# The last level of a block-triangular inverse on 64 x 64 blocks, and packed Q tiles, in a gated delta rule

## The chip, the cores and the metric

The kernel runs on one core of a Trainium2 chip. The metric is the device time of one execution in microseconds; a lower one is better. TensorE (PE) multiplies, VectorE (DVE), ScalarE (ACT) and GpSimd (POOL) work on tiles in on-chip memory, and PE writes its results into PSUM, eight banks of which the other engines read.

## What is computed

An attention layer, a feed-forward layer, a token mixer and a second feed-forward layer, over 512 tokens of 1024 features, all in float32. The change is in the mixer, in its gated delta rule. It has 8 heads of 128 features, and for each head and chunk of tokens a unit lower triangular system is solved:

```python
kk = jnp.einsum('nbhik,nbhjk->nbhij', kc, kc)
a_mat = jnp.where(strict, bc[..., :, None] * kk * decay, 0.0)
rhs = jnp.concatenate([bc[..., None] * vc, (bc * jnp.exp(gc))[..., None] * kc], axis=-1)
sol = lax.linalg.triangular_solve(a_mat + eye, rhs, left_side=True, lower=True,
                                  unit_diagonal=True)
...
def step(S, xs):
    q_i, qk_i, u_i, w_i, k_i, gl_i = xs
    v_new = u_i - jnp.einsum('bhck,bhkv->bhcv', w_i, S)
    o_i = jnp.einsum('bhck,bhkv->bhcv', q_i, S) + jnp.einsum('bhij,bhjv->bhiv', qk_i, v_new)
    S = S * jnp.exp(gl_i)[..., None, None] + jnp.einsum('bhck,bhcv->bhkv', k_i, v_new)
    return S, o_i
```

Ahead of it stand a causal convolution of width 4 and a SiLU over q, k and v; behind it a norm, a gate and projections.

## The kernel before

The large projections are products in which each float32 operand is split into a high and a low part, three matmuls for one (`acc<-hT,whi`, `acc<-hT,wlo` in the trace). They run all through the mixer. Between them a planner (`later`, `spend`, `run_until`) puts the small steps of the delta rule: each step that is set up gets a due time on a clock that the planner adds up from the matmuls issued so far, and is issued when that time has come. The table `DL` holds the delays: 10 us from U's first form to the first level of the inverse (`U`), 3.5 us between its steps (`lev`). That sets the program order, which PE keeps. The order on the other engines is set by a scheduler that looks at the whole program and moves instructions within an engine.

The kernel takes the tokens in 4 chunks of 128 (NT = 4). For each head, `decays` and `exps` make the decay matrices E and ET, `products` and `products2` the norms and E, the strictly triangular matrix of the system (L1119). `substitution` inverts its 16 x 16 diagonal blocks on DVE (shuffles into La, products pr, sums xs), and `expand` writes them into U, a tile of 128 x 512 with the four chunks side by side (L1169). `inverse(lev)` then joins neighbouring blocks of size s = 16, 32 and 64 into blocks of twice the size. A level has these steps: four matmuls with the chunk of E as the weights, onto the odd blocks' columns of U; DVE multiplies the result by a mask and writes Q (L1186); four transposes of U (L95) and their copy to X by ACT (L1190); then in `second` four matmuls of X and Q, and DVE subtracts them from U (L1195). A float32 matmul appears in the trace as two records, so `sc<-U,E x8` is four matmuls; a transposition is one.

Q of each level is a tile of its own, `Q_[lev]`, cleared once at the start of the mixer; the columns between the odd blocks stay zero. X comes anew from the work pool, which has 61 places of 128 x 512 (`self.tile`). The masks lie in `cst`, read from memory by one transfer. Around the inverse of head h stand the work of head h + 1, among it `ev_conv`: ACT copies a projection to cvr and scales it to cvy, DVE adds three taps (L1048, widths 511, 510 and 509), and ACT applies the SiLU (L1050).

Of the kernel before, what the change touches and what calls it, by code (L numbers as in the profile page):

```python
# [12 lines left out]
ALU = mybir.AluOpType  # L13
AX = mybir.AxisListType

P = 128
S = 512
NT = S // P
# [15 lines left out]
DL = dict(ada=21.24, qk=11.18, p0=10.0, wt=6.0, o=14.0, U=10.0, hn=7.73, lev=3.5, ch=2.2, cs=25.33, po=13.74, pr=18.0, T=3.17, la=6, gs=4, gp=5, Ts=6.12, P2=150)  # L34
# [7 lines left out]
class Net:  # L42
# [607 lines left out]
    def attention_layer(self):  # L650
# [17 lines left out]
        def qk(g, which):  # L668
# [17 lines left out]
            def evict(t, bank):  # L686
# [4 lines left out]
                ss = sp.tile([P, 8], F32, tag="ss8", name="ss8")  # L691
                nc.vector.tensor_reduce(ss, sq.rearrange("p (h d) -> p h d", d=64), axis=AX.X, op=ALU.add)
                r = self.rstd(ss, 8, 64)
# [58 lines left out]
        def attn(g, total):  # L752
# [48 lines left out]
            def weigh(h, b, wt, rs):  # L801
# [13 lines left out]
                ss = sp.tile([P, NT], F32, tag="ss4", name="ss4")  # L815
                nc.vector.tensor_reduce(ss, sq.rearrange("p (b n) -> p b n", b=NT), axis=AX.X, op=ALU.add)
                r = self.rstd(ss, NT, P)
# [136 lines left out]

    def mixer(self):
        nc, a, sp = self.nc, self.a, self.sp
        H = 8
        win = a["mix_w_in_2"][0]
        C = self.const
        sl = lambda t: slice(t * P, (t + 1) * P)  # L960
        ch = lambda x: x.rearrange("p (t n) -> p t n", t=NT)
# [1 line left out]
        small = lambda name, n=NT: sp.tile([P, n], F32, tag=f"sm{n}", name=name, bufs=24 if n == NT else 4)  # L963

        cst = self.tile("cst")
        nc.gpsimd.dma_start(cst[:, :448], a["k_mix"])
        tri, bmask = cst[:, 0:128], cst[:, 128:256]
        mq = [cst[:, 256 + 64 * i:320 + 64 * i] for i in range(3)]
        cols, rows = self.cols, self.rows
        cw = cols[:, 11:107].rearrange("p (j n) -> p j n", j=4)  # L970
        dng, psc, delta0, rcnt_ = cols[:, 107:108], cols[:, 108:112], cols[:, 112:128], cols[:, 128:192]
        alog, dtb = rows[:, 256:264], rows[:, 264:272]
        Q_ = [self.tile(f"Q{i}") for i in range(3)]
        for q in Q_:
            nc.gpsimd.memset(q, 0.0)


        G = lambda name: C.tile([P, H, NT], F32, name=name)
        beta, gc, egc = G("beta"), G("gc"), G("egc")
        gdram = self.dram.tile([H, S], F32, name="gdram")  # L980
        fl = lambda x: x.rearrange("p h t -> p (h t)")
# [7 lines left out]
        def ba_trans(ba):  # L989
# [10 lines left out]
            nc.vector.reciprocal(beta, e)  # L1000
            nc.vector.tensor_tensor(y, v[:, 8:16, :], dtb.unsqueeze(2).broadcast_to([P, H, NT]), op=ALU.add)
            nc.vector.tensor_scalar(t1, y, 0.0, None, op0=ALU.min)
# [15 lines left out]
            nc.gpsimd.tensor_tensor(ea, work[:, 192:200], alog, op=ALU.pow)  # L1018
            nc.vector.scalar_tensor_tensor(y, y, -1.0, ea.unsqueeze(2).broadcast_to([P, H, NT]), op0=ALU.mult, op1=ALU.mult)

# [37 lines left out]
        def mm4(out, a_, b_, t0=0, cols=lambda x: x):  # L1058
            for t in range(t0, NT):
                self.mm(cols(out[:, sl(t)]), a_[:, sl(t)], cols(b_[:, sl(t)]))  # L1060

        def delta(h):
            yq, yk, yv = conv_out[h], conv_out[8 + h], conv_out[16 + h]
            d = {}
# [22 lines left out]
            def products():  # L1087
# [6 lines left out]
                nc.scalar.activation(sq, trk, AF.Square)  # L1094
                nc.vector.tensor_reduce(ssq[:, NT:], ch(sq), axis=AX.X, op=ALU.add)
                trq = self.bank("sc")
                self.transpose4(trq, lambda t: yq[:, sl(t)])
                sq = self.tile("sq")
                nc.scalar.activation(sq, trq, AF.Square)
                nc.vector.tensor_reduce(ssq[:, 0:NT], ch(sq), axis=AX.X, op=ALU.add)  # L1100
                nc.vector.tensor_scalar(ssq, ssq, EPS, None, op0=ALU.add)
# [36 lines left out]
            def substitution():  # L1138
# [4 lines left out]
                Ac = sp.tile([P, NT, 16], F32, tag="Ac", name="Ac", bufs=1)  # L1143
                nc.vector.tensor_reduce(Ac, tmp.rearrange("p (t b j) -> p t j b", t=NT, b=8), axis=AX.X, op=ALU.add)
                La = [self.tile("La").rearrange("p (i t j) -> p i t j", i=8, t=NT) for _ in range(2)]
# [20 lines left out]
                def expand():  # L1166
                    U = self.tile("U")
                    b8 = lambda x, n: x.unsqueeze(n).broadcast_to([P, NT, 8, 16])
                    nc.vector.tensor_tensor(U.rearrange("p (t b i) -> p t b i", t=NT, b=8), b8(xs, 2),  # L1169
                                            b8(bmask.rearrange("p (b i) -> p b i", b=8), 1), op=ALU.mult)  # L1170
                    d["U"] = U
                    self.later(DL["U"], lambda: inverse(0))
# [2 lines left out]

            def inverse(lev):

                s = 16 << lev
                odd = lambda x: x.rearrange("p (u two s) -> p u two s", two=2, s=s)[:, :, 1, :]
                A, U, Q = d["E"], d["U"], Q_[lev]  # L1180
                qp = self.bank("sc")
                mm4(qp, A, U, cols=odd)
                na = 4 // (1 << lev)
                msk = mq[lev].rearrange("p (a s) -> p a s", s=s).unsqueeze(1).broadcast_to([P, NT, na, s])
                v4 = lambda x: x.rearrange("p (t a two s) -> p t a two s", t=NT, two=2, s=s)[:, :, :, 1, :]
                nc.vector.tensor_tensor(v4(Q), v4(qp), msk, op=ALU.mult)  # L1186
                xp = self.bank("sc")
                self.transpose4(xp, lambda t: U[:, sl(t)])
                X = self.tile("X")
                nc.scalar.copy(X, xp)  # L1190

                def second():
                    up = self.bank("sc")
                    mm4(up, X, Q, cols=odd)
                    nc.vector.tensor_tensor(odd(U), odd(U), odd(up), op=ALU.subtract)  # L1195
                    self.later(DL["lev"], (lambda: inverse(lev + 1)) if lev < 2 else weights)

                self.later(DL["lev"], second)

# [62 lines left out]
        def zcol(h):  # L1262
            og_[h] = self.tile("z")
            self.gemm_col(win[:, 3584 + h * P:3584 + (h + 1) * P], KD, self.hmov,
                          lambda bank: nc.scalar.activation(og_[h], bank, AF.Silu))
# [37 lines left out]
        def yacol(n):  # L1303
            self.gemm_col(a["pool_proj_2"][0, :, n * P:(n + 1) * P], 4, lambda k: yT[k],
                          lambda bank: nc.vector.tensor_tensor(m1[n], bank, m1[n], op=ALU.mult))

        cols = (4608, 512, 512 + 1024, 512 + 2048)
# [12 lines left out]
        zcol(0)  # L1320
        for h in range(H):
            if h:
# [15 lines left out]
        for n in range(KD):  # L1338
            yacol(n)
        self.run_until(lambda: st["og"] == H)  # L1340
        oT = [self.hp.tile([P, KD, S], F32R, tag=f"hT{i}", name=f"oT{i}") for i in range(2)]
# [55 lines left out]
def constants():  # L1397

    import numpy as np

    p = np.arange(P)[:, None]
    f = np.arange(P)[None, :]
    d = p + (S - P) - np.arange(S)[None, :]
    def pairs(s):
        m = (p // s % 2 == 0) & (f // s == p // s + 1)
        return m.reshape(P, -1, 2, s)[:, :, 1, :].reshape(P, 64)

    c = {
        "k_ident": p == f,
        "k_d3": np.where(d >= 0, -d, NEG),  # L1410
        "k_mix": np.concatenate([p <= f, p // 16 == f // 16] + [pairs(s) for s in (16, 32, 64)], 1),
    }
    return {n: np.ascontiguousarray(v.astype(np.float32)) for n, v in c.items()}

# [36 lines left out]
```

## Time and profile before

| | us |
|---|---|
| median of 3 runs | 1855.97 |
| lowest and highest run | 1852.57, 1855.99 |
| the profiled execution | 1854.37 |
| its span, first to last instruction | 1852.6 |
| PE busy in the span | 1811.6 |
| DVE, ACT, POOL busy | 1405.9, 934.2, 409.2 |

The mean granted TensorE clock of the execution is 0.996 of full speed. The time of an execution is its span and 1.8 us around it. The mixer's inverses lie between 1056 and 1350 us. In the timeline a row gives the start, the time from the start of the first to the end of the last of its instructions, the engine, the line, the operation with what it writes and reads, and how many there were; in square brackets stands for how long the engine sat idle ahead of it and who ended that. Ends of matmuls are modelled and overlap the next ones, so distances between starts are the safer reading.

### The profile page before, as it was taken

The page shows a single profiled execution, that of the slowest core. Times are in us where ns is not written, and L with a number is a line of the kernel's source. Part 1 is how long each engine was busy: PE and PEld are TensorE (multiplying, and loading weights), DVE is VectorE, ACT ScalarE, POOL GpSimd, SP SyncE. Part 2 cuts the span into 40 slices and gives each one's busy share as a digit, 9 for nine tenths or more (in the row PEclk, how much of TensorE's full clock was granted, in tenths as well). Part 3 has the DMA queues.
Part 4 walks back from the last instruction along what each step waited for, and adds up shares of the span by engine and source line. Part 5 has one row for each costly group of instructions (what it writes and reads, how often), then busy time and mean ns, then how long its engine had stood idle before and what let it go on. Part 6 is the DMA issues. An engine that isn't in the chain of part 4 may idle for free. (4 is left out here: it accounts for less than half of the span.)

```text
span 1852.6 us, 29069 instructions
## 1 busy us (share of the span) xinstructions
PE 1811.6 (98%) x10799; PEld 1598.0 (86%) x10799; DVE 1405.9 (76%) x2904; ACT 934.2 (50%) x1696; POOL 409.2 (22%) x396
## 2 busy tenths in 40 slices
PE   8999999999999999999999999999999999999997
PEld 5888888888888999998898778888888899999886
DVE  5558777777856899998365798787868789999833
ACT  5576676475743544453245745654433254445421
POOL 3213124042102123232030212212110022322201
PEclk9999999999999999999999999999999999999999
DMA  4535544535422233357324321222357323333731
GB/s 171 136 107 144 161 120 126 188 92 154 133 86 73 69 115 95 112 187 234 114 62 121 88 65 52 63 63 77 100 170 231 117 69 114 94 113 103 228 103 57
DMA packets 186594, 217.93 MB, mean 118 GB/s; under 512 B 9619, under 2 KB 129827, under 8 KB 186453
## 3 DMA queue, kind: packets, MB, share of 16 engines
q1 hardware_dynamic: 178864, 192.68, 34.6%
q0 software_dynamic: 6864, 22.27, 3.9%
q8 instruction: 85, 1.39, 0.3%
q10 hardware_dynamic: 724, 1.12, 0.2%
q14 instruction: 57, 0.46, 0.1%
HBM read 201.34 MB, written 2.11 MB: 110 GB/s over the span
## 5 line engine op out<-in xcount | busy, mean ns | idle before, releaser
L84 PE MATMUL acc<-hT,whi 128*128 128x256 f32 (+1 forms) x2704 | 639.9, 330 | 0.6 <-DVE hT L107 0.5
L84 PEld LDWEIGHTS acc<-hT,whi 128*128 128x128 f32 x2704 | 445.5, 191 | 33.4 <-DVE hT L107 0.7
L84 PE MATMUL acc<-hT,wlo 128*128 128x256 f32 (+1 forms) x1352 | 440.3, 326 | 3.0 <-DVE wlo L107 2.9
L106 ACT CAST whi<-raw 128x1024 fp32r<-128x1024 f32 (+1 forms) x325 | 285.7, 880 | 296.3 <-PE acc L84 232.2
L107 DVE TENSOR_TENSOR wlo<-raw,whi 128x1024 fp32r<-128x1024 f32 (+1 forms) x325 | 330.5, 1027 | 132.1 <-ACT whi L106 130.6
L84 PEld LDWEIGHTS acc<-hT,wlo 128*128 128x128 f32 x1352 | 257.5, 190 | 26.1 <-DVE wlo L107 4.2
L84 PE MATMUL acc<-whi,hT 128*128 128x512 f32 x768 | 264.9, 403 | 1.9 <-ACT hT L106 1.9
L84 PE MATMUL acc<-whi,gs 128*128 128x512 f32 x704 | 219.6, 390 | 1.6 <-DVE gs L107 1.6
L305 POOL TENSOR_TENSOR rs<-ms,mhalf 128x8 f32<-128x8 f32 (+2 forms) x60 | 86.2, 1438 | 447.5 <-DVE ms L303 388.0
L84 PE MATMUL acc<-T,whi 128*128 128x256 f32 x960 | 174.5, 283 | 0.0
L84 PEld LDWEIGHTS acc<-whi,hT 128*128 128x128 f32 x768 | 144.1, 188 | 32.1 <-ACT hT L106 2.9
L84 PEld LDWEIGHTS acc<-whi,gs 128*128 128x128 f32 x704 | 132.0, 188 | 29.9 <-DVE gs L107 2.5
L106 ACT CAST whi<-S 128x512 fp32r<-128x512 f32 x160 | 99.4, 621 | 115.2 <-DVE S L232 87.7
L84 PE MATMUL acc<-wlo,hT 128*128 128x512 f32 x384 | 150.5, 392 | 2.8 <-DVE wlo L584 2.8
L84 PEld LDWEIGHTS acc<-T,whi 128*128 128x128 f32 x960 | 149.8, 192 | 0.0
L107 DVE TENSOR_TENSOR wlo<-S,whi 128x512 fp32r<-128x512 f32 x160 | 140.1, 895 | 0.2 <-ACT whi L106 0.2
L84 PE MATMUL acc<-wlo,gs 128*128 128x512 f32 x352 | 137.1, 389 | 0.0
L84 PE MATMUL acc<-T,wlo 128*128 128x256 f32 x480 | 135.8, 283 | 0.0
L232 POOL TENSOR_TENSOR S<-raw,S 128x512 f32<-128x512 f32 x40 | 65.7, 1643 | 200.7 <-DVE S L232 158.6
L780 ACT ACTIVATE p<-p,mn 128x128 f32<-128x128 f32 (+3 forms) x128 | 71.1, 557 | 48.8 <-DVE mn L776 48.2
L84 PEld LDWEIGHTS acc<-T,wlo 128*128 128x128 f32 x480 | 92.2, 192 | 0.0
L84 PEld LDWEIGHTS acc<-wlo,hT 128*128 128x128 f32 x384 | 72.5, 189 | 14.7 <-DVE wlo L584 3.7
(299 smaller groups left out, 3113.6 us busy)
## 6 DMA issues: line engine op xcount, KB each, us to landing
raw<-in_ffn_w_in_dram SPq DMA_DIRECT2D x88, 512.0 KB, 3.6
raw<-in_l_w_in_dram SPq DMA_DIRECT2D x60, 512.0 KB, 4.1
raw<-in_mix_w_in_dram SPq DMA_DIRECT2D x53, 512.0 KB, 3.9
araw<-in_ada_w_dram SPq DMA_DIRECT2D x96, 256.0 KB, 4.3
raw<-in_ffn_w_out_dram SPq DMA_DIRECT2D x44, 512.0 KB, 3.7
ada<-in_ada_w_dram POOLq DMA_DIRECT2D x48, 256.0 KB, 4.2
raw<-in_l_w_out_dram SPq DMA_DIRECT2D x16, 512.0 KB, 3.7
ab<-in_ada_b_dram POOLq DMA_DIRECT2D x18, 256.0 KB, 4.2
```

The costliest lines, as they stand in the source:

```text
L84: self.nc.tensor.matmul(out, a, b, start=start, stop=stop, skip_group_check=onto)
L106: return (self.nc.scalar.copy(hi, src), self.nc.vector.tensor_tensor(lo, src, hi.bitcast(F32), op=ALU.subtract))
L107: self.nc.vector.tensor_tensor(lo, src, hi.bitcast(F32), op=ALU.subtract))
L232: sub = lambda o, x, y, op=ALU.subtract, e=nc.vector: e.tensor_tensor(o, x, y, op=op)
L305: pin(nc.gpsimd.tensor_tensor(r[:, :n], ms[:, :n], self.mhalf[:, :n], op=ALU.pow))
L780: nc.scalar.activation(p_[m][:, :L], p_[m][:, :L], AF.Exp, bias=mn[:, m:m + 1], scale=-1.0, accum_out=st[:, m, b:b + 1])
```

## The change

The first two levels stay in `inverse(lev)`, but Q and X both come from the work pool, and Q is packed: the odd blocks of a chunk lie side by side, 64 columns for each chunk, 256 in all. The three tiles Q_ and their clearing on POOL go.

The last level is a new function, `inverse_halves`. With the rows and columns of a chunk cut into a low and a high half, it multiplies the lower left quarter of E with the lower right quarter of U (64 x 64 weights, 64 columns), copies the result to Q without a mask, transposes the upper left quarter of U alone, and subtracts the product from the upper right quarter of U. Its tiles are 64 x 256. The third mask is no longer read.

```diff
@@ -954,7 +954,7 @@
 
     def mixer(self):
         nc, a, sp = self.nc, self.a, self.sp
-        H = 8
+        H, H2 = 8, P // 2
         win = a["mix_w_in_2"][0]
         C = self.const
         sl = lambda t: slice(t * P, (t + 1) * P)
@@ -963,16 +963,13 @@
         small = lambda name, n=NT: sp.tile([P, n], F32, tag=f"sm{n}", name=name, bufs=24 if n == NT else 4)
 
         cst = self.tile("cst")
-        nc.gpsimd.dma_start(cst[:, :448], a["k_mix"])
+        nc.gpsimd.dma_start(cst[:, :384], a["k_mix"])
         tri, bmask = cst[:, 0:128], cst[:, 128:256]
-        mq = [cst[:, 256 + 64 * i:320 + 64 * i] for i in range(3)]
+        mq = [cst[:, 256 + 64 * i:320 + 64 * i] for i in range(2)]
         cols, rows = self.cols, self.rows
         cw = cols[:, 11:107].rearrange("p (j n) -> p j n", j=4)
         dng, psc, delta0, rcnt_ = cols[:, 107:108], cols[:, 108:112], cols[:, 112:128], cols[:, 128:192]
         alog, dtb = rows[:, 256:264], rows[:, 264:272]
-        Q_ = [self.tile(f"Q{i}") for i in range(3)]
-        for q in Q_:
-            nc.gpsimd.memset(q, 0.0)
 
 
         G = lambda name: C.tile([P, H, NT], F32, name=name)
@@ -1175,25 +1172,52 @@
 
             def inverse(lev):
 
-                s = 16 << lev
+                s, na = 16 << lev, 4 >> lev
                 odd = lambda x: x.rearrange("p (u two s) -> p u two s", two=2, s=s)[:, :, 1, :]
-                A, U, Q = d["E"], d["U"], Q_[lev]
+                A, U = d["E"], d["U"]
+                Q, X = self.tile("Q")[:, :NT * H2], self.tile("X")
+                v4 = lambda x: x.rearrange("p (t a s) -> p t a s", t=NT, s=s)
+                q = lambda x, t: x[:, t * H2:(t + 1) * H2].rearrange("p (a s) -> p a s", s=s)
                 qp = self.bank("sc")
-                mm4(qp, A, U, cols=odd)
-                na = 4 // (1 << lev)
+                for t in range(NT):
+                    self.mm(q(qp, t), A[:, sl(t)], odd(U[:, sl(t)]))
                 msk = mq[lev].rearrange("p (a s) -> p a s", s=s).unsqueeze(1).broadcast_to([P, NT, na, s])
-                v4 = lambda x: x.rearrange("p (t a two s) -> p t a two s", t=NT, two=2, s=s)[:, :, :, 1, :]
-                nc.vector.tensor_tensor(v4(Q), v4(qp), msk, op=ALU.mult)
+                nc.vector.tensor_tensor(v4(Q), v4(qp[:, :NT * H2]), msk, op=ALU.mult)
                 xp = self.bank("sc")
                 self.transpose4(xp, lambda t: U[:, sl(t)])
-                X = self.tile("X")
                 nc.scalar.copy(X, xp)
 
                 def second():
                     up = self.bank("sc")
-                    mm4(up, X, Q, cols=odd)
+                    for t in range(NT):
+                        self.mm(odd(up[:, sl(t)]), X[:, sl(t)], q(Q, t))
                     nc.vector.tensor_tensor(odd(U), odd(U), odd(up), op=ALU.subtract)
-                    self.later(DL["lev"], (lambda: inverse(lev + 1)) if lev < 2 else weights)
+                    self.later(DL["lev"], (lambda: inverse(lev + 1)) if lev < 1 else inverse_halves)
+
+                self.later(DL["lev"], second)
+
+            def inverse_halves():
+
+                A, U = d["E"], d["U"]
+                Q, X = (self.tile(n)[:H2, :NT * H2] for n in ("Q", "X"))
+                lo, hi = slice(0, H2), slice(H2, P)
+                h = lambda x, t: x[lo, t * H2:(t + 1) * H2]
+                qp, xp = self.bank("sc"), self.bank("sc")
+                for t in range(NT):
+                    self.mm(h(qp, t), A[hi, sl(t)][:, lo], U[hi, sl(t)][:, hi])
+                nc.vector.tensor_copy(Q, qp[lo, :NT * H2])
+                for t in range(NT):
+                    nc.tensor.transpose(h(xp, t), U[lo, sl(t)][:, lo], self.ident[lo, lo])
+                    self.now += 0.06
+                nc.scalar.copy(X, xp[lo, :NT * H2])
+
+                def second():
+                    up = self.bank("sc")
+                    for t in range(NT):
+                        self.mm(h(up, t), h(X, t), h(Q, t))
+                    u = ch(U)[lo, :, hi]
+                    nc.vector.tensor_tensor(u, u, up[lo, :NT * H2].rearrange("p (t n) -> p t n", t=NT), op=ALU.subtract)
+                    self.later(DL["lev"], weights)
 
                 self.later(DL["lev"], second)
 
@@ -1408,7 +1432,7 @@
     c = {
         "k_ident": p == f,
         "k_d3": np.where(d >= 0, -d, NEG),
-        "k_mix": np.concatenate([p <= f, p // 16 == f // 16] + [pairs(s) for s in (16, 32, 64)], 1),
+        "k_mix": np.concatenate([p <= f, p // 16 == f // 16] + [pairs(s) for s in (16, 32)], 1),
     }
     return {n: np.ascontiguousarray(v.astype(np.float32)) for n, v in c.items()}
```

DVE at the start of head 1's work, where head 0 is in the first level of its inverse. Before, Q of head 0 stands first; E, abd, kd, Ac, kt, cvy and La are head 1's:

```order
L1186 TENSOR_TENSOR Q_10010<-sc,cst 128x16x16
L1085 TENSOR_TENSOR er<-cvy,er 128x512
L1095 TENSOR_REDUCE ssqk<-sq 128x4
L1100 TENSOR_REDUCE ssqk<-sq 128x4
L1101 TENSOR_SCALAR ssqk<-ssqk 128x8
L1119 SCALAR_TENSOR_TENSOR E<-sc,b_11008,E 128x128 x4
L1142 TENSOR_TENSOR abd<-E,cst 128x512
L1125 TENSOR_TENSOR kd<-kt,ekd 128x512
L1144 TENSOR_REDUCE Ac<-abd 128x64
L1126 TENSOR_TENSOR kt<-kt,bB 128x512
L1048 SCALAR_TENSOR_TENSOR cvy<-cvr,cols,cvy 128x511
L1153 STREAM_SHUFFLE La<-Ac 128x64
```

After, from the second convolution tap of the same stretch on (the E x4, abd, kd, Ac, kt and the first tap stand ahead of these rows as they did before):

```order
L1150 STREAM_SHUFFLE La<-Ac 128x64
L1045 SCALAR_TENSOR_TENSOR cvy<-cvr,cols,cvy 128x510
L1150 STREAM_SHUFFLE La<-Ac 128x64
L1045 SCALAR_TENSOR_TENSOR cvy<-cvr,cols,cvy 128x509
L1150 STREAM_SHUFFLE La<-Ac 128x64
L1185 TENSOR_TENSOR Q<-sc,cst 128x256
L1150 STREAM_SHUFFLE La<-Ac 128x64 x12
L1158 TENSOR_TENSOR pr<-La,xs 128x4x7
L1158 TENSOR_TENSOR pr<-La,xs 128x4x8
L1194 TENSOR_TENSOR U<-U,sc 128x16x16
```

Q has moved from ahead of E to behind the third tap (128x509), and the subtraction from U stands behind the rest of the shuffles and two products.

ACT at the same place, before. X belongs to head 0, cvr, cvy and vb to head 1:

```order
L1044 COPY cvr<-acc 128x512
L1046 ACTIVATE cvy<-acc,cols 128x512
L1190 COPY X<-sc 128x512
L1135 ACTIVATE vb<-sc,bv 128x128 x4
L1050 ACTIVATE cvy<-cvy 128x512
L106 CAST whi<-raw 128x1024
```

And after:

```order
L1041 COPY cvr<-acc 128x512
L1043 ACTIVATE cvy<-acc,cols 128x512
L1047 ACTIVATE cvy<-cvy 128x512
L1188 COPY X<-sc 128x512
L1132 ACTIVATE vb<-sc,bv 128x128 x4
L106 CAST whi<-raw 128x1024
```

The copy to X stands behind the SiLU of cvy (the line of 128x512 without cols), which was two rows behind it.

PE at the third level of head 0, before; the first two rows of U are the first half of the level:

```order
L95 MATMUL sc<-ident,cvy 128x128 x8
L84 MATMUL sc<-U,E 128x64 x4
L95 MATMUL sc<-ident,U 128x128 x4
L84 MATMUL acc<-hT_9847,whi 128x512
L84 MATMUL acc<-hT_9848,whi 128x512
L84 MATMUL acc<-hT_9847,wlo 128x512
```

After:

```order
L95 MATMUL sc<-ident,cvy 128x128 x8
L84 MATMUL sc<-U,E 64x64 x4
L1210 MATMUL sc<-ident,U 64x64 x4
L84 MATMUL acc<-hT_9847,whi 128x512
L84 MATMUL acc<-hT_9848,whi 128x512
L84 MATMUL acc<-hT_9847,wlo 128x512
```

The same number of instructions stands there, on 64 x 64 blocks. Up to here PE's order is that of before, with the packed forms of Q in the first two levels.

## Rows read from the trace of the kernel before

**Rows 1.** The page: engines' busy us (share of the span) and instructions

```profile
PE 1811.6 (98%) x10799; PEld 1598.0 (86%) x10799; DVE 1405.9 (76%) x2904; ACT 934.2 (50%) x1696; POOL 409.2 (22%) x396
```

**Rows 2.** PE's waits, 1000 to 1400 us: releaser, then total us, times, longest

```profile
PE sc L84 <- DVE U L1169: 2.7, 1, 2.7
PE sc L84 <- DVE Q L1186: 2.2, 2, 1.9
PE sc L84 <- DVE U L1195: 2.1, 1, 2.1
```

**Rows 3.** Windows: PE, PEld, DVE, ACT, POOL busy, granted clock, DMA, GB/s

```profile
1058.40:1061.80 3.40, 3.40 (x11) 2.81 (x12) 1.84 (x4) 2.02 (x4) 1.44 (x1) 0.50 0.56 154
1072.00:1075.50 3.50, 3.50 (x13) 3.02 (x13) 3.50 (x12) 0.56 (x2) 0.00 (x0) 0.51 0.53 143
1096.10:1099.50 3.40, 3.36 (x22) 3.11 (x23) 3.40 (x34) 1.52 (x3) 0.00 (x0) 1.00 0.00 0
```

**Rows 4.** Timeline of PE, head 0: start, us, instruction, [idle before <-releaser]

```profile
1056.74 1.08 PE L84 MATMUL sc<-U,E 128*128 128x64 f32 x8 [2.68 <-DVE U L1169]
...
1063.89 1.00 PE L84 MATMUL sc<-Q,X 128*128 128x64 f32 x8
...
1068.68 0.39 PE L84 MATMUL acc<-hT,wlo 128*128 128x512 f32 x1
1071.20 1.22 PE L84 MATMUL sc<-U,E 128*128 128x64 f32 x8 [2.14 <-DVE U L1195]
```

**Rows 5.** Timeline of DVE at the same place

```profile
1057.86 0.42 DVE L1186 TENSOR_TENSOR Q<-sc,cst 128x256 f32<-128x256 f32 x1
...
1062.63 1.13 DVE L1119 SCALAR_TENSOR_TENSOR E<-sc,b,E 128x128 f32<-128x128 f32 x4 [2.36 <-POOL b L1107]
...
1068.16 0.74 DVE L1048 SCALAR_TENSOR_TENSOR cvy<-cvr,cols,cvy 128x509 f32<-128x509 f32 x1
```

**Rows 6.** Timeline of ACT at the same place

```profile
1059.79 0.63 ACT L1190 COPY X<-sc 128x512 f32<-128x512 f32 x1
...
1068.99 0.63 ACT L1050 ACTIVATE cvy<-cvy 128x512 f32<-128x512 f32 x1 [5.49 <-DVE cvy L1048]
```

**Rows 7.** Timeline of PE at head 0's third level

```profile
1083.51 1.00 PE L84 MATMUL sc<-U,E 128*128 128x64 f32 x8
...
1084.72 0.71 PE L84 MATMUL acc<-hT,whi 128*128 128x512 f32 x2
...
1089.25 1.00 PE L84 MATMUL sc<-Q,X 128*128 128x64 f32 x8
1090.07 0.71 PE L84 MATMUL acc<-hT,whi 128*128 128x512 f32 x2
```

**Rows 8.** Timeline of PE at two small tiles (16 rows, then 32 columns)

```profile
961.02 0.40 PE L84 MATMUL acc<-hT,whi 128*128 128x256 f32 x2
961.26 0.28 PE L84 MATMUL acc<-hT,wlo 128*128 128x256 f32 x1
961.47 0.42 PE L992 MATMUL sc<-ident,ba 16*128 16x16 f32 x4
...
962.16 0.28 PE L84 MATMUL acc<-hT,wlo 128*128 128x256 f32 x1
...
990.10 0.62 PE L84 MATMUL acc<-hT,whi 128*128 128x512 f32 x2
990.56 0.40 PE L84 MATMUL acc<-hT,wlo 128*128 128x512 f32 x1
990.79 0.27 PE L1030 MATMUL sc<-ident,gc 128*32 128x128 f32 x1
...
991.37 0.40 PE L84 MATMUL acc<-hT,wlo 128*128 128x512 f32 x1
```

**Rows 9.** PE's loads at the 16-row tile: timeline, then line L992 (ns min/median/max)

```profile
961.47 0.32 PEld L992 LDWEIGHTS sc<-ident,ba 16*128 16x128 f32 x4
...
L992 PEld LDWEIGHTS sc<-ident,ba x4: 133/137/138, 961.5 to 961.6; 16*128 16x128 f32 x4
```

## The prediction

> **What bounds the kernel now.** First the busy times of the engines: TensorE (PE) is busy for 98% of the span [rows 1], so what counts is the work that PE does and the moments at which it waits; DVE, ACT and POOL have idle time, and a longer or shorter instruction of theirs counts only where PE waits for it. So the next view is the list of PE's waits over the stretch in which all eight heads are inverted (1000 to 1400 us). Three lines name the inverse: 2.7 us for the first U, 2.1 us for the U of the next level, 2.2 us for a Q, of which 1.9 in one wait [rows 2]. All of them lie in heads 0 and 1. After that, up to the last head, the list holds almost nothing: from head 2 on the inverse is covered by projection matmuls, and only PE's own work in it is on the path.
>
> Third, the table of windows, for the granted clock. In the 3.4 us after the 2.7 us wait the granted clock is 0.50 (1.2 GHz in place of 2.4), in the 3.5 us after the 2.1 us wait 0.51, and after the 1.9 us wait it stays 1.00 [rows 3]. So each of the two longer waits also costs about half of the window behind it, 1.7 us: PE did in 3.4 us what takes 1.7 at 1.00.
>
> Last the timeline around head 0. PE runs the first U x E at 1056.74, Q x X at 1063.89 without waiting, projection matmuls until 1069.07 (5.18 us from the start of Q x X), then waits and goes on with the second level at 1071.20 [rows 4].
>
> **The change, part by part.** *The order of DVE and ACT at head 0.* PE keeps its order up to the third level of head 0, but the other engines' order comes from the scheduler, and there the change moves two instructions a long way. Q of the first level is evicted by DVE at 1057.86 before, as an early instruction; after, it stands behind the whole start of head 1 (the four E, abd, kd, Ac, kt and three convolution taps). On ACT, X is copied at 1059.79 before; after, it stands behind the SiLU of the convolution, which waits for the third tap. Whether the scheduler does so because the tile Q now has to be found in the work pool I can't tell from the order; that it does is what counts, since the queue of each engine is worked off in order. The third tap ran at 1068.16 for 0.74 and the SiLU behind it for 0.63 from 1068.99 [rows 5, 6]. The taps stand behind E, which waited for POOL; without the 0.42 us of Q in front, the two reductions that POOL waits for come 0.4 earlier, so I take the third tap to end at 1068.5, the SiLU at 1069.15 and X (0.63 [rows 6]) at 1069.75; Q is done by then (1068.5 + 0.42 = 1068.9). PE, which stands at Q x X at 1063.89, goes on at about 1069.8: **a new wait of 5.9 us**. Behind it on PE are queued the projection matmuls, which need nothing from DVE, and nothing on PE can pass it.
>
> What is late next? The second level needs U, which DVE subtracts behind the remaining twelve shuffles and two products; DVE is there at about 1071.3 and the product of Q and X has been done since 1070.7, while PE has its 5.18 us of projections to do until 1075.0. So the 2.14 us wait at 1071.20 is gone. PE starts the second level at 1075.0 in place of 1071.20, 3.8 us late. Before, the half clock behind the 2.14 us wait then cost 1.7 us; that goes with the wait: 3.8 - 1.7 = 2.1. The new wait of 5.9 us is longer than both that were followed by a half clock, so I charge it one such window, +1.7 (0 to 1.7). **Order at head 0: +3.8 us** (2.1 to 5).
>
> *Later heads.* At head 1, PE waited 1.9 us for Q [rows 2]; DVE is still the later one there, and what feeds DVE at that place comes from PE and POOL and shifts with PE. I take the wait as unchanged. From there to head 2 the order puts Q and U somewhat later on DVE than before relative to PE (3 to 7 us, when its instructions are laid out with the durations of before), in a stretch with waits of none to 0.5 us. I charge 0.5 us, between 0 and 2.5 (one more wait of the size of the 1.9 us one, with a bit). From head 3 on the order of DVE is no later than before.
>
> *PE's work in the third level.* Before, it is 8 records of U x E and 4 transposes from 1083.51 to 1084.72, 1.21 us, and 8 records of Q x X from 1089.25 to 1090.07, 0.82 us [rows 7]: 2.03 us per head for 20 records, 0.10 each. The records are the same in number after, with weights of 64 rows by 64 columns in place of 128 by 128 and, for the transposes, 64 columns moving in place of 128. The trace has no such operation. The nearest rows on the low side are the four 16-column transposes of the gates, whose loads follow each other every (0.32 - 0.137) / 3 = 0.061 us [rows 9]; on the high side, the pitch stays at 0.10. I take 0.06, since both the loaded columns and the moving ones are fewer or equal: 1.2 us per head, **a saving of 0.8** (0 to 1.0, the latter for half of 0.10).
>
> Against this stand two visits per head to a smaller tile of the array. The trace has two such visits. At the gates the time from one wlo record to the next around four 16-row transposes is 962.16 - 961.26 = 0.90, of which three records of 0.12 are normal; 0.54 remain, less four transposes at 0.061 to 0.10: 0.14 to 0.30 for going there and back. At the transposition of gc, with 32 columns, 991.37 - 990.56 = 0.81, less three records at 0.23 and one transposition at 0.10: 0.02 [rows 8]. A 64 x 64 tile narrows rows and columns, so I take the row with fewer rows as nearest, 0.25 per visit, 0.5 per head, with 0.02 and 0.30 as the ends. A rule of the Trainium skill ("TensorEngine Tiling (Array Packing)", Tiling Modes, Key Properties) says that changing the tiling mode, not the tile alone, drains TensorE. The first of the two visits agrees with it, the second shows nearly no drain. By the rule at the larger price the saving per head would be 0.2, by the second visit 0.8.
>
> Net per head: 0.8 - 0.5 = 0.3. Head 0's is lost, since PE waits for DVE at head 1; seven heads give **-2.1 us**. The ends are -7 (seven heads at 1.0 with visits at 0.02) and +4.2 (seven heads at 0 with visits at 0.30).
>
> *The rest.* The evictions of the third level get smaller on DVE (64 partitions, no mask) and ACT (256 columns in place of 512); between U x E and Q x X lie 4.5 us of projections [rows 7] in which both finish anyway, so nothing. The packed Q of the first two levels changes neither the number nor the width of matmuls: nothing on PE. Three memsets on POOL and 64 columns of one DMA lie long ahead of their users: nothing, and no cover is lost.
>
> **Sum:** +3.8 + 0.5 - 2.1 = +2.2 us against the profiled execution of 1854.37 us: 1856.6. That execution lies 1.6 us under the median of the runs (1855.97), so the forecast as a median is 1858.2; I say 1858.
>
> **The rivals.**
> *Faster: the blocks pay in full.* If a visit costs 0.02 as at gc and 64 columns take half the pitch, PE saves 1.0 per head, 7 us over seven heads. With +4.3 from the order this is -2.7 us, with a smaller wait at head 0 (no half clock, +2.1) -4.9: 1851 to 1853. For it: the gc row. Against: the gates' row. Chance 0.16.
> *Slower: the late evictions go on.* The mechanism: after the 5.9 us wait, Q or X of heads 1 and 2 also come late, as the order has them 3 to 7 us later on DVE, and PE waits twice more for about 2 us with a half clock behind each. It decides from a wait of over 2 us, the least that was followed by a half clock [rows 3]. Price 2 x (2 + 1.7) = 7.4 in place of 0.5: +9 us, 1865; with one such wait 1861. For it: PE has only some 5 us of projections between the levels of those heads. Against: DVE idled for 2.36 us ahead of E [rows 5], so it has some air. Chance 0.2.
> *Slower: 64 columns are no shorter.* Pitch stays 0.10 and visits cost 0.25: +4 us where I have -2.1, 1864. For it: the matmul records before move 64 columns already, so their pitch may not be set by what is loaded. Against: the loads at the gates. Chance 0.12.
> *The first wait doesn't come*, because DVE or ACT are much earlier there than I worked out: then -2.1 - 0.7 and no more, 1853. Chance 0.05, as the order leaves no way round the third tap.
> The forecast itself: 0.47.
>
> **How the numbers follow.** A difference under 0.2% (3.7 us) can hardly be told from none here. Faster than 1852.3 are most of the first rival and a little of the others: 0.14. Slower than 1859.7 are nearly all of the second and third rivals (0.3) and a small part of the forecast's own case: 0.34. Within: 0.52. The range of 1851 to 1864 leaves out about 0.1 at the top (two long waits with half clocks) and under 0.1 at the bottom.
>
> **What would show it right or wrong.** In the profile after: among PE's waits one of 5 to 6.5 us at the first Q x X of head 0, released by ACT's X or DVE's Q; no wait at the second level of head 0; a granted clock near 0.5 for about 3.4 us behind the new wait. PE's records of the third level: 12 of them in about 0.7 us plus the visit, 8 in about 0.5 plus the visit, where the sum of both is 2.03 before; if it is over 2.0, the blocks bring nothing, if it is 1.1 the visits are free. The forecast is wrong if X of head 0 is copied before the SiLU on ACT, if a wait of over 2 us stands at heads 1 or 2, or if the sum of the third level is outside 1.4 to 2.0.

## The result and the profile after

The change is slower: 1877.4 us (median of 4 runs, 1875.29 to 1880.72) against 1855.98 of before, a ratio of 1.0122, interval 1.011 to 1.0134. The profiled execution took 1875.29 us, its span is 1873.5, 20.9 more than before.

The engines' busy times and the chain in the page after, to be held against [rows 1]:

```profile
PE 1818.3 (97%) x10799; PEld 1596.5 (85%) x10799; DVE 1408.5 (75%) x2904; ACT 932.8 (50%) x1696; POOL 409.3 (22%) x393
PE 80%; DVE 11%; ACT 3%; issue 3%; DMA 2%; POOL 1%; SPq 0%; POOLq 0%; DVEq 0%; ACTq 0%
```

PE is as much the bound as before, but its share of busy time fell: it waits more. The list of PE's waits, 1000 to 1450 us, after (releaser, total us, times, longest):

```profile
PE sc L84 <- ACT X L1188: 7.8, 2, 6.0
PE tr L84 <- DVE S L1252: 3.9, 2, 2.2
PE sc L84 <- DVE Q L1208: 2.8, 1, 2.8
PE sc L84 <- DVE Q L1185: 2.8, 2, 2.1
PE sc L84 <- DVE U L1166: 2.7, 1, 2.7
PE sc L84 <- DVE U L1219: 1.8, 1, 1.8
PE acc L84 <- DVE wlo L107: 1.0, 1, 1.0
PE acc L84 <- DVE oT L107: 0.9, 1, 0.9
PE sc L84 <- ACT whi L106: 0.8, 1, 0.8
PE sc L84 <- DVE U L1194: 0.3, 1, 0.3
```

The sum is 24.8 us, where the list of before has 8.8 (of it 7.0 in [rows 2]): **16.0 us of new waits**. Where they stand shows PE's timeline after; these are the starts at which PE had waited over 1.5 us:

```profile
1056.96 1.52 PE L84 MATMUL sc<-U,E 128*128 128x64 f32 x8 [2.66 <-DVE U L1166]
...
1069.97 1.97 PE L84 MATMUL sc<-Q,X 128*128 128x64 f32 x8 [5.97 <-ACT X L1188]
...
1129.29 1.10 PE L84 MATMUL sc<-Q,X 128*128 128x64 f32 x8 [1.83 <-ACT X L1188]
...
1177.89 0.49 PE L84 MATMUL tr<-S,wT 128*128 128x128 f32 x2 [1.67 <-DVE S L1252]
...
1229.22 0.65 PE L84 MATMUL sc<-Q,X 64*64 64x64 f32 x8 [2.81 <-DVE Q L1208]
...
1309.05 0.49 PE L84 MATMUL tr<-S,wT 128*128 128x128 f32 x2 [2.21 <-DVE S L1252]
...
1325.86 0.94 PE L84 MATMUL sc<-U,kt 128*128 128x128 f32 x6 [1.75 <-DVE U L1219]
...
1343.75 1.59 PE L84 MATMUL sc<-Q,X 128*128 128x64 f32 x8 [2.13 <-DVE Q L1185]
```

The wait of head 0 is the one forecast (5.97 us, PE goes on at 1069.97; the forecast was 5.9 and 1069.8). It alone isn't the result: waits run on to 1344 us, in the last heads, where before has none over 0.4. Some of them have a stretch at half clock behind them (windows after, with the columns of [rows 3]; the third number from the end is the granted clock):

```profile
1070.00:1073.40 3.40, 3.40 (x12) 3.11 (x13) 2.44 (x21) 1.43 (x5) 0.00 (x0) 0.50 0.02 5
1310.20:1316.60 6.40, 6.40 (x26) 4.88 (x25) 4.11 (x38) 2.51 (x8) 0.00 (x0) 0.50 0.00 0
1344.00:1347.00 3.00, 3.00 (x11) 1.97 (x11) 1.08 (x2) 0.00 (x0) 0.54 (x1) 0.52 0.05 14
```

Half of the time that PE is busy at the half clock is lost: 9.1 us in the mixer after and 3.4 before, **5.7 more**. (The granted clock is at 0.5 for 20.5 us of the mixer after, and PE stands waiting for X in 2.3 of them.) 16.0 + 5.7 = 21.7, and the work of PE in the last levels got about 2.4 us shorter (below), which leaves 19.3 of the 20.9. The sum tells where PE's time went, not what each wait is worth: a wait can take in a half clock or a wait ahead of it.

That work, at one head (PE, then its loads, then PE at the second half of the level), where [rows 7] has that of before:

```profile
1144.94 0.39 PE L84 MATMUL av<-vn,kd 128*128 128x128 f32 x2
1145.25 0.68 PE L84 MATMUL sc<-U,E 64*64 64x64 f32 x8
1145.86 0.41 PE L1210 MATMUL sc<-ident,U 64*64 64x64 f32 x4
1146.20 0.73 PE L84 MATMUL acc<-hT,whi 128*128 128x512 f32 x2
```

```profile
1145.25 0.54 PEld L84 LDWEIGHTS sc<-U,E 64*64 64x64 f32 x8
1145.86 0.25 PEld L1210 LDWEIGHTS sc<-ident,U 64*64 64x64 f32 x4
```

```profile
1149.99 0.40 PE L84 MATMUL acc<-hT,wlo 128*128 128x512 f32 x1
1150.32 0.68 PE L84 MATMUL sc<-Q,X 64*64 64x64 f32 x8
1150.92 0.73 PE L84 MATMUL acc<-hT,whi 128*128 128x512 f32 x2
```

The starts of single records in the trace are 0.058 us apart in the groups of eight and 0.056 in the transposes (the first distance of a group is longer, 0.107 and 0.081), where they were 0.11. Between the groups the distance is larger by about 0.09: 0.327 from the last wlo to Q x X, where a wlo record otherwise takes 0.23; 0.149 from U x E to the transposes, and 0.146 to 0.149 on leaving. The level takes 0.95 + 0.60 us (1146.20 - 1145.25, 1150.92 - 1150.32) and 0.09 twice on entering, 1.73 in place of 2.03: 0.3 per head, 2.4 for eight.

### The profile page after: what moved, and what is told of

Its sections match the earlier page's. It is cut to its first block, busy times and chain, and to the rows that moved or that the text cites. A ratio compares the mean times of both kernels' runs of the same rounds, so it can differ in the third digit from the quotient of the medians.

```text
span 1873.5 us, 29069 instructions
## 1 busy us (share of the span) xinstructions
PE 1818.3 (97%) x10799; PEld 1596.5 (85%) x10799; DVE 1408.5 (75%) x2904; ACT 932.8 (50%) x1696; POOL 409.3 (22%) x393
## 4 chain that ended last, share of the span: by engine, by line
PE 80%; DVE 11%; ACT 3%; issue 3%; DMA 2%; POOL 1%; SPq 0%; POOLq 0%; DVEq 0%; ACTq 0%
PE acc L84 70%; PE sc L84 4%; DVE wlo L107 2%; PE av L84 2%; PE sc L95 1%; DMA araw<-in_ada_w_dram 1%; PE tr L95 1%; PE tr L795 1%; DVE cvy L1045 1%; POOL rqk L1100 1%; ACT whi L106 1%; DVE S L232 1%; PE tr L84 1%; DVE hn L346 0%; DVE pr L1158 0%
## 5 line engine op out<-in xcount | busy, mean ns | idle before, releaser
L84 PEld LDWEIGHTS acc<-wlo,hT 128*128 128x128 f32 x384 | 72.8, 189 | 14.4 <-DVE wlo L584 3.3
```

The source lines that it names most:

```text
L84: self.nc.tensor.matmul(out, a, b, start=start, stop=stop, skip_group_check=onto)
```

## Experiments

Three things differ at once in the change: the blocks, the tiles of Q (packed, and drawn from the shared work pool), and one number, the 0.06 us that the planner is charged for a small transposition where a large one is charged 0.11. With it the planner's clock stands 0.2 us per head behind what it was, and so PE's rows move: 1014 of the 10799 records are others than before in the same place, the first at 1090 us. In every run with 0.11 PE's rows are those of before one for one. Theory A is that the loss comes from the orders and the blocks gain a little; the rivals are B, the blocks themselves cost, and C, that drawing Q from the pool does it and not the packing.

### The blocks alone

Against before: the block code for the last level, with Q of that level in the third permanent tile, and the charge of before.

```diff
-                    self.later(DL["lev"], (lambda: inverse(lev + 1)) if lev < 2 else weights)
+                    self.later(DL["lev"], (lambda: inverse(lev + 1)) if lev < 1 else inverse_halves)
...
+                Q, X = Q_[2][:H2, :NT * H2], self.tile("X")[:H2, :NT * H2]
...
+                    self.now += 0.11
```

> The last level works on 64 x 64 blocks; Q of the first two levels stays strided in its permanent cleared tiles, the last level's Q in the third one, and the planner charges 0.11 us for each small transposition as it did for a large one, so that PE's order is that of before to the row, and DVE's and ACT's nearly so. Theory A (the loss comes from the orders, the blocks gain a little: 0.606 + 0.340 + 0.605 us per head in place of 2.03, less about 0.1 on entering and leaving): 1 to 3 us faster than before, PE's list of waits as before (2.7, 2.2, 2.1 us). Theory B (the blocks themselves cost, by the changes of tile): slower than before by 3 us or more, with waits as before.

1853.58 us against 1854.52, a ratio of 0.9995 (0.9986 to 1.0004). PE's waits of head 0 and 1 are those of before (2.69, 2.20, 2.04). The 0.9 us lie just under A's range and within what can't be told from nothing; B, which asked for 3 us or more of loss, falls.

### The planner's number

First on the kernel with the blocks (0.06 in place of 0.11), then on the kernel before, where it is the only edit and the work is the same to the instruction:

```diff
                 self.transpose4(xp, lambda t: U[:, sl(t)])
+                if lev == 2:
+                    self.now -= 0.2
```

> As the run with the blocks alone, but the planner charges 0.06 us for a small transposition, as in the change: 0.2 us less on its clock per head. Theory A: head 0 as before, but at head 6 U is subtracted some 30 rows later on DVE, so PE waits there for S and U and runs at half clock behind it: 8 to 12 us slower than the blocks alone. Theory B: no difference from the blocks alone.

> The kernel before, on whole chunks, with one number changed: the planner is charged 0.2 us less for the four transpositions of each head's last level. The work is the same to the instruction. Theory A (the planner's charge alone brings the waits of head 6): 8 to 12 us slower than before, with waits of about 2 us for S and U near 1310 to 1325 us and the granted clock near 0.5 behind them. Theory B (the blocks cost): as before.

The first took 1864.35 us, 10.8 more than the blocks alone, and with the waits for S, Q, S and U too (2.64, 2.82, 2.20 and 1.67). The second took 1865.02 against 1855.74, a ratio of 1.0054 (1.004 to 1.0068), 9.3 us slower. PE's waits in the second that are over 1.4 us, behind the one for the first U (2.65, as before):

```profile
1069.65 1.10 PE L84 MATMUL sc<-U,E 128*128 128x64 f32 x8 [3.78 <-DVE U L1197]
...
1171.53 0.49 PE L84 MATMUL tr<-S,wT 128*128 128x128 f32 x2 [2.27 <-DVE S L1230]
...
1223.07 1.07 PE L84 MATMUL sc<-Q,X 128*128 128x64 f32 x8 [2.68 <-DVE Q L1186]
...
1304.00 0.49 PE L84 MATMUL tr<-S,wT 128*128 128x128 f32 x2 [2.21 <-DVE S L1230]
...
1317.75 0.94 PE L84 MATMUL sc<-U,kt 128*128 128x128 f32 x6 [1.50 <-DVE U L1197]
```

The last four are four of the change's waits, at S, Q, S and U, within 0.6 us of their size there. A is right on the time and on the waits, but not on the clock: behind the waits at 1304 and 1317 the granted clock stays 1.00, and in the first run too; it is at 0.5 at 1071 and 1225 us. The mechanism is in DVE's timeline of this run: S, for which PE waits, stands behind the whole start of the next head, and its first instruction, the four E, waits for POOL.

```profile
1299.24 1.13 DVE L1119 SCALAR_TENSOR_TENSOR E<-sc,b,E 128x128 f32<-128x128 f32 x4 [2.34 <-POOL b L1107]
1300.29 0.68 DVE L1123 TENSOR_TENSOR ET<-sc,ET 128x512 f32<-128x512 f32 x1
1300.89 0.68 DVE L1142 TENSOR_TENSOR abd<-E,cst 128x512 f32<-128x512 f32 x1
1301.48 0.68 DVE L1125 TENSOR_TENSOR kd<-kt,ekd 128x512 f32<-128x512 f32 x1
1302.09 1.00 DVE L1144 TENSOR_REDUCE Ac<-abd 128x64 f32<-128x512 f32 x1
1303.00 0.68 DVE L1126 TENSOR_TENSOR kt<-kt,bB 128x512 f32<-128x512 f32 x1
1303.60 0.34 DVE L1230 SCALAR_TENSOR_TENSOR S<-S,egl,av 128x128 f32<-128x128 f32 x1
```

Before, the same E and S on DVE, and PE behind that S:

```profile
1293.57 0.35 DVE L1119 SCALAR_TENSOR_TENSOR E<-sc,b,E 128x128 f32<-128x128 f32 x1 [0.46 <-POOL b L1107]
...
1294.59 0.86 DVE L1119 SCALAR_TENSOR_TENSOR E<-sc,b,E 128x128 f32<-128x128 f32 x3
...
1301.36 0.34 DVE L1228 SCALAR_TENSOR_TENSOR S<-S,egl,av 128x128 f32<-128x128 f32 x1
```

```profile
1301.76 0.49 PE L84 MATMUL tr<-S,wT 128*128 128x128 f32 x2 [0.35 <-DVE S L1228]
```

That S stands behind kt too, but E was over by 1295.5 and had made DVE wait only 0.46 us, and PE waited 0.35 us for S. The change has the rows of this run in the same order, the six lines from E to kt and then S at 1308.65. The wait for Q at head 4's last level has the same source, though Q has hardly moved on DVE (one row): E, which stands ahead of it, waits 2.34 us for POOL's b in the change and in this run, and not at all before.

### Packed Q

Only the packing, in all three levels, on whole chunks with the third mask: once in three permanent tiles, once from the work pool. The packing is that of the change's first two levels.

```diff
-                Q, X = self.tile("Q")[:, :NT * H2], self.tile("X")
+                Q, X = Q_[lev][:, :NT * H2], self.tile("X")
```

> Only the packing of Q, in all three levels, in three permanent tiles; the last level on whole chunks with its mask. Theory A (the packing, not the place in the pool, lets the scheduler put Q 18 rows and X one row later at head 0; rows of heads 2 to 7 as before): one wait of about 6 us for X at head 0 with a half clock behind it, 3 to 6 us slower than before. Theory C (the place in the pool does it): as before, no wait for X.

> Only the packing of Q, in all three levels, with Q from the work pool; the last level on whole chunks with its mask. Theory A: the wait of 6 us at head 0 and one or two of about 2 us at heads 1 to 3, where Q stands 18 rows late once more: 5 to 9 us slower than before, and nothing of the waits at head 6. Theory C: 5 to 9 us slower than before, where the same in permanent tiles is not.

In permanent tiles 1856.25 us, 1.001 (1.0001 to 1.0019), 1.7 us slower; from the pool 1868.9, 1.0077 (1.0063 to 1.0091), 14.4 slower. Both have the long wait at head 0:

```profile
1068.19 1.97 PE L84 MATMUL sc<-Q,X 128*128 128x64 f32 x8 [6.01 <-ACT X L1189]
```

This is the run with the permanent tiles, in which the wait costs 1.7 us (interval 0.2 to 3.5), less than its own length: the waits of 2.1 and 1.9 us behind it [rows 2] are gone. So A is right that packing without the pool can bring the wait at head 0 (packed Q in places of its own, below, doesn't have it), and wrong that this is most of what the packing from the pool costs. The other 12.7 us need the pool, as C said. In the run with the pool further waits stand from head 2's last level to head 7 (1.29, 1.81, 0.95, and the longest, 3.56, at the first level of the last head):

```profile
1337.79 1.08 PE L84 MATMUL sc<-Q,X 128*128 128x64 f32 x8 [3.56 <-DVE Q L1185]
```

DVE shows why this one is so long. Q, nine rows later than before, now stands behind a row of another part of the program (`aacc`) that waits for its weights from memory; before, Q is done at 1323.5, ahead of that row. In the change it stands there too, at 1343.18.

```profile
1334.58 0.49 DVE L475 TENSOR_SCALAR aacc<-araw,silu_c 128x512 f32<-128x512 f32 x1 [1.04 <-DMA araw<-in_ada_w_dram]
...
1337.23 0.41 DVE L1185 TENSOR_TENSOR Q<-sc,cst 128x256 f32<-128x256 f32 x1
```

### The change with the planner's old number, and with priority

The change with 0.11 in place of 0.06:

> The change with one number altered: the planner charges 0.11 us for each small transposition. Theory A: the waits at head 6 (S, U) are gone, those of heads 0 to 3 (X, Q) stay: 4 to 8 us slower than before, 12 to 16 faster than the change. Theory B: within 3 us of the change.

1869.11 us, 1.0073 (1.0057 to 1.0088): 13.4 slower than before, so beyond the 4 to 8 that A gave, and 8.3 faster than the change where A gave 12 to 16. The waits for S and U at 1309 and 1326 are gone as it said; what is left is about what the pool costs (the run with only the packing from the pool: 14.4), the longest again for Q of the last head (4.29).

Priority in the scheduler for the evictions of the inverse, in the change and, with the old number, in the blocks alone (one of the six places):

```diff
-                nc.scalar.copy(X, xp)
+                with self.tc.high_priority(offset=PRIO):
+                    nc.scalar.copy(X, xp)
```

> The change with the evictions of Q and X and the subtraction from U given priority in the scheduler, in all levels; the planner's charge stays 0.06. X of head 0 is ahead of the SiLU again, as is U ahead of the shuffles; Q of head 0 stays 14 rows late, and at head 6 U stands 5 rows late in place of 31. Theory A: X no longer waits, Q still does at head 0: 3 to 8 us slower than before, most of the loss of head 6 gone. Theory B: within 3 us of the change.

> The blocks alone (strided Q, the planner's charge 0.11) with priority for the evictions of the inverse; Q, X and U stand up to 14 rows earlier on DVE than before. Theory A: the wait of 2.1 us at the second level of head 0, and the half clock behind it, go in part: 2 to 6 us faster than before. Theory B: slower than before by 2 us or more.

1870.76 us, 1.0085 (1.0071 to 1.0099), and 1855.85, 1.0001 (0.9992 to 1.0009). In neither run does either theory hold: the first is 15.0 us slower than before and 6.6 faster than the change, the second 0.1 slower than before. In the first, X is early again, but Q isn't, and PE waits 5.36 us for it at the same place; S still costs 2.26 and 1.92. In the second the wait at 1068 stays (2.08), and a new one of 3.13 for X of head 1's last level appears. PE comes to head 1's first Q x X 35.0 us after the first U x E, where the blocks alone need 39.3, but that X keeps its place on ACT, behind the SiLU of the next convolution and a table load of 1.28 us. Nearly all of the 4.3 us is lost again in that wait and the half clock behind it.

### Q in places of its own

Q drawn from a small pool of its own: for the packing alone, and for the whole change with the old number.

```diff
-        self.wk = pool("wk", SLOTS)
+        self.wk = pool("wk", SLOTS - 3)
+        self.qp_ = pool("qq", 3)
...
-                Q, X = self.tile("Q")[:, :NT * H2], self.tile("X")
+                Q, X = self.qp_.tile([P, NT * H2], F32, tag="q", name="Q"), self.tile("X")
```

> Only the packing of Q, in all three levels, with Q from a small pool of its own (three places of 128 x 256, the work pool three places smaller); the last level on whole chunks with its mask. Q, X and U then stand at the same rows of DVE and ACT as before, for all heads. Theory A2 (not the packing, but drawing Q from the shared work pool changes the orders): within 2 us of before, no wait for X, where the same with Q from the work pool was 14 us slower. Theory D (packed operands themselves cost on PE or DVE): slower than before by 3 us or more with waits as before.

> The whole change (64 x 64 blocks in the last level, packed Q) with two things altered: Q comes from a small pool of its own, and the planner charges 0.11 us for a small transposition. The rows of Q, X and U stand as before within 4. Theory A2: as the blocks alone, 0 to 3 us faster than before, so that 20 us or more of the change's loss were the pool and the planner's number. Theory D: slower than before by 3 us or more.

1857.78 us, 1.0014 (1.0004 to 1.0023), and 1857.2, 1.0013 (1.0004 to 1.0022): no wait for X, and 12 us of the pool's cost gone, but 2 to 3 us slower than before. That is neither of the two theories. PE's timeline shows the loss in the attention stage, 700 us ahead of the inverse, in both; here the packing alone:

```profile
346.56 0.50 PE L85 MATMUL sc<-qkT 128*128 128x512 f32 x1 [0.48 <-DVE mn L777]
...
348.85 0.41 PE L796 MATMUL tr<-ident,p 128*128 128x128 f32 x2 [1.56 <-DVE p L786]
```

Before runs there without a wait. The attention stage draws from the same work pool, and with 58 places its instructions stand in another order on DVE from 341 us on; in the mixer of the first run the order on PE, DVE and ACT is that of before. So the last run leaves the work pool its 61 places and gives Q one:

```diff
+        self.qp_ = pool("qq", 1)
```

> The whole change with the planner's charge at 0.11 us and Q in one place of its own (128 x 256), while the work pool keeps its 61 places; in the run before this one it had 58, and the attention stage, far ahead of the mixer, waited 2 us more at 345 to 349 us. DVE's order in the attention stage is then that of before again, as is the order in the mixer. Theory A3 (all of the change's loss is order: the pool's places, also in the attention stage, and the planner's number): as the blocks alone, 0 to 3 us faster than before, with waits as before in both stages. Theory D (packed Q costs something itself): 2 us or more slower than before, as with the own pool of three places.

1852.79 us against 1854.64, 0.9992 (0.9983 to 1.0001). This is the whole change, with its blocks and packed Q, with one number and one pool altered: 1.9 us faster than before by the medians, its interval just reaching 1. D falls. On PE, DVE and ACT its instructions stand in the order of the blocks alone, row for row, so what it has more than that run is packed Q, and what it has less than the change is the two altered orders. Of all kernels run it is the fastest against its own runs of before, but that it beats before is not shown beyond the interval.

## Why the prediction was wrong

The forecast was 1858, the range up to 1864; measured were 1877.4. Step by step:

- **The new wait at head 0: right.** 5.9 us forecast, 5.97 measured, released by X behind the SiLU, and the wait of the second level is gone. Its price, +3.8, was too high by the run that has little else (+1.7): a wait that is followed by smaller ones takes them in, here that of head 1 too, which I had left standing. In that run's trace head 1's first Q x X starts 41.8 us after the first U x E of head 0, in place of 39.4 before.
- **PE's work in the last level: right.** Forecast 0.06 per record, 0.5 for tile changes, 0.3 saved per head; measured 0.058, 5 x 0.09 and 0.3. The visit that I took as nearest, the one with 16 rows [rows 8], was the right one. The Trainium skill ("TensorEngine Tiling (Array Packing)", Tiling Modes, Key Properties) says that changing the tiling mode, and not just the tile, drains TensorE. The trace has about 0.09 us at each of five changes per head. Four of them change the mode and agree; one is from one 64 x 64 tile to another, and there the trace differs from the page: the change of tile alone costs as much.
- **The later heads: this step failed.** I charged 0.5 us, with 2.5 as the bound, and wrote that from head 3 on DVE's order is no later than before. It is later: the subtraction of U at head 6's last level stands 31 rows further down, Q of head 7's first level nine, and where the rows have hardly moved they stand behind an E that comes later. The six waits of 0.8 to 2.8 us from 1177 to 1344 us, 11.4 in all, are the larger part of the 16. Heads 1 and 2, for which the 0.5 was meant, stay inside the bound: 0.67 at head 1 in place of 1.91, 1.83 and 0.32 at head 2. The prediction shows no row for the sentence on head 3 and later, and gives the shift of PE's rows behind head 0 no term at all. Of the signs that it named for being wrong none came, since they all lie in heads 0 to 2 and in the work of the third level.
- **What I didn't see at all** is that the shifts come from two separate sources. The line `self.now += 0.06` looks like bookkeeping; without any other edit it costs 9.3 us. The line that draws Q from the pool, against a place of its own, costs the rest: 1869.11 against 1852.79, with ratios to before of 1.0073 and 0.9992. The sum of the separate runs, 9.3 + 14.4 - 0.9 = 22.8, is close to the 21.4 measured, so they add up with little overlap.
- **The rival "late evictions go on"** had the mechanism right (waits of about 2 us at later heads, half clocks behind some), with 1865 as its price and a chance of 0.2. It was held to heads 1 and 2; it went on to head 7.
- **The price of a half clock: wrong, without weight in the sum.** The prediction has each of the two long waits before cost 1.7 us more by the half clock behind it, and takes 1.7 off and adds 1.7 for head 0. At head 0 nothing shows that cost. Before, PE is at half clock behind the first wait [rows 3]; in the last run of the experiments it isn't, and it only waits longer at the next place, where DVE sets the time. Behind the second wait PE runs at half clock for 5.1 us there, in place of 3.4 before, and its wait for Q of head 1 is the shorter for it (1.28 in place of 1.91). Before, then that last run (three rows of PE, then windows with the columns of [rows 3]):

```profile
1096.14 1.08 PE L84 MATMUL sc<-Q,X 128*128 128x64 f32 x8 [1.91 <-DVE Q L1186]
```

```profile
1055.36 1.08 PE L85 MATMUL sc<-U,E 128*128 128x64 f32 x8 [2.65 <-DVE U L1167]
...
1069.80 1.97 PE L85 MATMUL sc<-U,E 128*128 128x64 f32 x8 [3.73 <-DVE U L1195]
...
1094.74 1.08 PE L85 MATMUL sc<-Q,X 128*128 128x64 f32 x8 [1.28 <-DVE Q L1186]
```

```profile
1055.00:1060.00 5.00, 4.57 (x28) 3.89 (x29) 3.84 (x8) 4.05 (x8) 1.03 (x1) 1.00 0.37 107
1069.80:1074.90 5.10, 5.10 (x18) 4.61 (x19) 5.00 (x18) 1.53 (x3) 0.00 (x0) 0.50 0.36 103
```

From the first U x E to head 1's Q x X it is 39.40 us before (from 1056.74 [rows 4]) and 39.38 here.

What stays open is why the scheduler puts Q and X later when Q comes from the work pool. The number of places in the work pool alone doesn't do it: with 58 and with 61, and Q outside it, the rows of Q, X and U in the mixer are those of before within 4. With Q in packed permanent tiles they are late at head 0 only, with a place of its own nowhere. How the scheduler's choice comes about the runs don't show.

## What to carry to other kernels

In a kernel whose order is made by a planner and a scheduler, compare the order on every engine from the change to the end, not only around it, and above all where a row that PE waits for has moved behind one that itself waits, for another engine or for a transfer. Let the signs of being wrong cover the whole stretch. Change one thing that sets the order at a time: a charge of 0.05 us in a planner, or a tile drawn from a shared pool, can cost several times what the edit is worth, and an edit that saves 2 us of work can be judged only when both are held still. A shared pool carries the effect far from the edit: taking three places from it cost 2 us in a stage 700 us earlier.

## What the runs showed of the hardware

The clock after a wait isn't settled by the length of the wait. In the kernel before, half clock followed waits of 2.7 and 2.1 us and not one of 1.9 [rows 3]. In the blocks with priority neither the wait of 2.69 nor that of 2.08 was followed by it, only the one of 3.13; in the blocks alone a wait of 2.04 was. I charged it to the longer waits by a rule that the runs don't bear out. Nor does a half clock always cost time: at head 0, where PE waits for DVE again a few us later, the stretch from the first U x E to head 1's Q x X takes 39.4 us with a half clock behind the first wait and without one.

A 64 x 64 transposition of float32 is one record, as a large one is, at 0.056 us in place of 0.11. The loads get shorter with the tile, but not in the same ratio: a load for U x E took 192 ns on 128 x 128 and 129 to 135 on 64 x 64, while the records follow each other at half the distance.
